# First norm by channels: x turned as it arrives, the roots spread by a matmul, and the mixer's residual read back from a stored copy

## Chip, cores, metric

The kernel runs on one core of a Trainium2 chip. The time is device microseconds of one execution; three runs of the kernel before are at hand. Beside them stands one profiled execution with its trace. The engines are PE (TensorE, matrix products), DVE (VectorE), ACT (ScalarE), POOL (GpSimd) and SP, whose queue issues most of the DMAs.

## What is computed

A stack of two residual layers over a stream of 1024 positions with 1024 channels, each layer followed by a gated feed-forward block, and a last norm. Only the beginning matters here: a norm, the input projection of the first mixer, and its output projection with the residual.

```python
def rmsnorm(x, g):
    y = x * lax.rsqrt(jnp.mean(x * x, axis=-1, keepdims=True) + EPS)
    return y * g

def even_mixer(x, w_in, ..., w_out):
    p = x @ w_in
    xa, ga, c_pre, b_post, vb = jnp.split(p, ...)        # 512 channels each
    xa = causal_depthwise_conv(xa, lru_conv_w, lru_conv_b)
    ya = rg_lru(xa, ...) * jax.nn.gelu(ga)
    yb = b_post * causal_depthwise_conv(c_pre * vb, sconv_w, sconv_b)
    return jnp.concatenate([ya, yb], axis=-1) @ w_out

h = x
h = h + even_mixer(rmsnorm(h, mix0_norm), ...)
h = h + conv_glu_ffn(rmsnorm(h, ffn_norm[0]), ...)
h = h + odd_mixer(rmsnorm(h, mix1_norm), ...)
h = h + conv_glu_ffn(rmsnorm(h, ffn_norm[1]), ...)
out = rmsnorm(h, final_norm)
```

## The kernel before, in words

**Operands.** All products take activations with channels on the 128 partitions and positions along the row: `AH` and `AL` hold, for each of eight chunks of 128 channels, the rounded high part and the rest of 1024 positions. Weights come as blocks of 1024 rows by 128 columns (512 KB) and are split in the same way into `wh` (a cast on ACT) and `wl` (a subtraction on DVE, both in L129). A block of the result is the sum of AH·wh, AL·wh and AH·wl over eight chunks: 24 products for a half of 512 positions (`proj_half`, products in L376). Weight blocks are loaded by the class `Weights` in a fixed plan (0xa0, 0ga0, 0cp0, 0vb0, 0bp0, 0xa1, ...; output blocks 0o00 to 0o07 and again 0o10 to 0o17); two raw blocks and three split pairs are held at a time, so the cast of a block waits for the last product with the block three before.

**The first norm** (class `Start`) works on x with positions on the partitions: eight tiles of 128 positions by 1024 channels. For each tile ACT squares and sums a row (`squares`, L433), DVE and ACT form the root (`root`, L438 to L442), DVE multiplies by root and gain in one pass over 1024 columns (`scale`, L446; the gain is one row broadcast to all partitions, a DMA of 512 KB, `g0`), PE turns the product in eight 128x128 transposes into two PSUM banks (`high`, L455), ACT casts the banks into AH (L459), and DVE subtracts for AL (`low`, L464). The order for the first four tiles is the string `START`; `warm` (L470) puts plain products of the identity into PE's queue. Positions 0 to 511 of the blocks xa and ga are computed in two quarters of 256 as the tiles come, then the other four tiles are worked on beside the first half of block 0cp0 (`second`, `beside`), then come the second halves of xa, ga and 0cp0.

**Behind it.** xa goes through a convolution of four taps (ACT L402, DVE L405) and is split into xh and xl (L369, L370); the gates ra and ix are products with the small gate weights gwa and gwx (L1345), which POOL clears (L1326), loads (L1330) and ACT and DVE split. 0vb and 0bp follow. Blocks of 1024 positions have two PSUM buffers (`big`), halves have four (`sml`). SBUF tiles of 128x1024 (`t4`) and 128x512 (`t2`) have four buffers each; the parameter rows, gwa and gwx, and the rows of the next stage's convolution weights are t2 tiles.

**The residual.** `out_proj0` computes the eight output blocks for positions 0 to 511, then for the rest. `residual(oc)` loads 128 channels of x (512 KB in rows of 512 bytes, L546), PE turns them in eight transposes (L550) and ACT copies the two banks into `hT` (L551), the stream with channels on the partitions. `evict` adds a block's result (L557), stores it to `hdr` in DRAM (L558) for a later stage, and squares it for the next norm.

**Order.** A planner traces the whole program and gives each engine its queue, by the order of the program among what is ready in its own model of time. An instruction inside `tc.issue_after(i)` stands behind i on the engine that the two share; it doesn't wait for i to end.

Of the kernel before, what the change touches and what calls it, by code (L numbers as in the profile page):

```python
# [16 lines left out]
P = 128  # L17
T = 1024
H = 512
# [35 lines left out]

START = "q0 r0 s0 q1 r1 s1 h0 q2 l0 r2 s2 h1 l1 w1 q3 r3 s3 h2 l2 w2 h3 l3".split()

WARM = {"h0": 3, "h1": 3}
# [25 lines left out]
class Weights:  # L84
# [12 lines left out]
    def _dma(self, n=None):  # L97
        n = n or NWST + (self.more is not None)
        while self.n_dma < min(self.n_conv + n, len(self.plan) if self.limit is None else self.limit):
# [6 lines left out]
            self.nc.sync.dma_start(w[:, :k, :m], ap)  # L106
# [13 lines left out]
    def ahead(self, depth=3):  # L120
# [14 lines left out]
        return did  # L135

# [20 lines left out]
def trunk(ctx: ExitStack, tc: tile.TileContext, x, mix0_norm, mix0_w_in, lru_conv_w, lru_conv_b,  # L157
# [258 lines left out]
    g0 = spl.tile([P, D], F32, name="g0")  # L416
    xs_, last = [], {}

    class Start:


        def __init__(self):
            self.ss = spl.tile([P, DC, 4], F32, name="sss")
            self.ys, self.ps = {}, {}

        def load(self, tt):
            xt = spl.tile([P, D], F32, tag="x", bufs=5, name=f"x{tt}")
            nc.sync.dma_start(xt, x[tt * P:(tt + 1) * P, :])
            xs_.append(xt)

        def squares(self, tt):
            y = self.ys[tt] = t4(f"xn{tt}")
            return act.activation(y, xs_[tt], AF.Square, accum_out=self.ss[:, tt, 0:1]), None  # L433

        def root(self, tt):
            sm = self.ss[:, tt]
            v, r, q = sm[:, 1:2], sm[:, 2:3], sm[:, 3:4]
            dve.tensor_scalar(v, sm[:, 0:1], 1.0 / D, EPS, op0=ALU.mult, op1=ALU.add)  # L438
            a = act.activation(r, v, AF.Abs_reciprocal_sqrt)
            dve.tensor_tensor(q, v, r, op=ALU.mult)  # L440
            dve.scalar_tensor_tensor(q, q, -0.5, r, op0=ALU.mult, op1=ALU.mult)
            return a, dve.scalar_tensor_tensor(r, q, 1.5, r, op0=ALU.add, op1=ALU.mult)  # L442

        def scale(self, tt):
            y = self.ys[tt]
            return None, dve.scalar_tensor_tensor(y, xs_[tt], self.ss[:, tt, 2:3], g0,  # L446
                                                  op0=ALU.mult, op1=ALU.mult)

        def high(self, tt):
            y, self.ps[tt] = self.ys.pop(tt), []  # L450
            for q_ in range(2):
                ps = psml(f"xp{tt}{q_}")
                for i in range(4):
                    c = 4 * q_ + i
                    pe.transpose(ps[:, i * P:(i + 1) * P], y[:, c * P:(c + 1) * P], ident)  # L455
# [11 lines left out]
        def warm(self, n):  # L467
            ps = psml("warm")
            for _ in range(n):
                pe.matmul(ps[:, :P], ident, ident, start=True, stop=True)  # L470
# [1417 lines left out]
```

## Time and profile before

| | |
|---|---|
| runs | 2139.49, 2139.52, 2137.47 us; median 2139.49 |
| profiled execution | 2138.28 us, its span 2136.6 us |
| granted PE clock, mean | 0.997 |
| PE busy | 2097.7 us (98%), 9673 products |
| DVE, ACT, POOL busy | 1599.6, 1068.9, 74.7 us |
| from HBM, to HBM | 181.93 MB, 64.26 MB |
| first product of the start (0xa) | 16.94 us |
| last product of the start (0cp0b) begins | 59.21 us |
| output projection, first product | 258.42 us |

Times in rows of the trace are us from the start of the span. A row of the timeline has start, duration, engine (PEld loads PE's stationary operand, SPq is SP's queue of DMAs), line of the kernel, operation, result<-operands, and, in brackets, how long the engine stood idle before it and what ended that. Products are pipelined: one is shown with some 0.39 us, and the next starts 0.23 us after it. A row by groups has the line, the names and shapes, count, busy time in us and mean ns. A row by stretches has the stretch, its length, busy time and instructions of PE, PEld, DVE, ACT and POOL, the granted PE clock, the DMA engines' share, and GB/s. A row of waits has who waited for whom, us in total, how often, and the longest.

### The profile page before, as it was taken

To read this page: it belongs to the slowest core of one execution; us is meant where nothing else is said; L and a number is where in the kernel's file an instruction comes from. 1 tells how busy PE (TensorE), PEld (TensorE's weight loads), DVE (VectorE), ACT (ScalarE), POOL (GpSimd) and SP (SyncE) were. 2 spreads that over 40 slices of the span, in tenths; PEclk is the share of its full clock that TensorE was granted. 3 is DMA by queue.
4 is the path that set the end of the run, shared out by engine and by line. 5 is a ranking of instruction groups with operands and counts; after the bars stand their busy time and mean duration, and the time that the engine had idled before them with its cause. 6 is when DMAs were issued, how large, how long until landed. Compare 5 with 4: busy or idle time off the path is not lost. (4 is left out here: it accounts for less than half of the span.)

```text
span 2136.6 us, 25861 instructions
## 1 busy us (share of the span) xinstructions
PE 2097.7 (98%) x9673; PEld 1721.0 (81%) x9673; DVE 1599.6 (75%) x2290; ACT 1068.9 (50%) x1493; POOL 74.7 (3%) x121
## 2 busy tenths in 40 slices
PE   8999999999999999999999999999999999999998
PEld 7888888788888878888778888788788888878887
DVE  6655647998888777876566666868998888777864
ACT  5333534654555555333556575744655545555323
POOL 0000001000000000000111111100000000000000
PEclk9999999999999999999999999999999999999999
DMA  4111342333333267751221211542233332267732
GB/s 149 57 50 43 109 150 94 101 107 109 103 108 94 79 223 248 238 168 69 75 67 46 82 48 58 165 151 89 94 116 106 104 109 95 85 234 244 232 101 79
DMA packets 269318, 249.98 MB, mean 117 GB/s; under 512 B 10224, under 2 KB 222000, under 8 KB 269192
## 3 DMA queue, kind: packets, MB, share of 16 engines
q1 hardware_dynamic: 268856, 247.83, 36.4%
q8 instruction: 76, 1.25, 0.2%
q0 software_dynamic: 192, 0.30, 0.1%
q14 instruction: 50, 0.41, 0.1%
q10 hardware_dynamic: 144, 0.20, 0.0%
HBM read 181.93 MB, written 64.26 MB: 115 GB/s over the span
## 5 line engine op out<-in xcount | busy, mean ns | idle before, releaser
L129 ACT CAST wh<-wst 128x1024 fp32r<-128x1024 f32 (+1 forms) x87 | 86.3, 992 | 222.6 <-PE op L376 45.0
L129 DVE TENSOR_TENSOR wl<-wst,wh 128x1024 fp32r<-128x1024 f32 (+1 forms) x87 | 99.9, 1148 | 96.2 <-ACT wh L129 96.0
L676 PE MATMUL X<-TH,wh 128*128 128x512 f32 x384 | 150.1, 391 | 1.8 <-ACT u L1033 1.4
L676 PE MATMUL X<-TH,wl 128*128 128x512 f32 x384 | 149.7, 390 | 0.7 <-DVE wl L370 0.7
L676 PE MATMUL X<-TL,wh 128*128 128x512 f32 x384 | 149.5, 389 | 0.0
L369 ACT CAST wh<-wst 128x1024 fp32r<-128x1024 f32 x96 | 100.3, 1051 | 75.7 <-PE YZ L676 49.5
L370 DVE TENSOR_TENSOR wl<-wst,wh 128x1024 fp32r<-128x1024 f32 x96 | 116.5, 1218 | 11.9 <-ACT wh L369 11.9
L698 DVE SCALAR_TENSOR_TENSOR cg<-g,par_c,cg 128x1023 f32<-128x1023 f32 x88 | 112.7, 1281 | 7.1 <-ACT cg L692 6.0
L698 DVE SCALAR_TENSOR_TENSOR cv<-v,par_c,cv 128x1023 f32<-128x1023 f32 (+1 forms) x88 | 112.3, 1276 | 0.1
L676 PE MATMUL YZ<-AH,wh 128*128 128x512 f32 x240 | 93.5, 389 | 0.0
L676 PE MATMUL YZ<-AL,wh 128*128 128x512 f32 x240 | 93.4, 389 | 0.0
L676 PE MATMUL YZ<-AH,wl 128*128 128x512 f32 x240 | 93.4, 389 | 0.0
L1033 ACT COPY u<-X 128x512 f32<-128x512 f32 x40 | 23.6, 589 | 136.3 <-PE X L676 136.3
L676 PEld LDWEIGHTS X<-TH,wh 128*128 128x128 f32 x384 | 72.1, 188 | 18.9 <-ACT u L1033 2.6
L676 PEld LDWEIGHTS X<-TH,wl 128*128 128x128 f32 x384 | 72.1, 188 | 16.5 <-DVE wl L370 1.6
L676 PEld LDWEIGHTS X<-TL,wh 128*128 128x128 f32 x384 | 72.1, 188 | 14.8
L376 PE MATMUL op<-AH,wh 128*128 128x512 f32 x192 | 76.3, 397 | 0.6 <-ACT hT_o L551 0.6
L376 PE MATMUL op<-AH,wl 128*128 128x512 f32 x192 | 74.8, 390 | 0.0
L376 PE MATMUL op<-AL,wh 128*128 128x512 f32 x192 | 74.8, 390 | 0.0
L692 ACT ACTIVATE cg<-g,par_c 128x1024 f32<-128x1024 f32 x44 | 54.8, 1246 | 30.0 <-DVE g L1057 25.6
L1055 DVE TENSOR_TENSOR v<-p,u 128x512 f32<-128x512 f32 x40 | 27.6, 690 | 53.9 <-ACT u L1048 53.9
L1598 ACT ACTIVATE P<-P,sm 128x128 f32<-128x128 f32 (+3 forms) x64 | 49.7, 777 | 30.0 <-DVE sm L1595 29.7
(779 smaller groups left out, 6309.3 us busy)
## 6 DMA issues: line engine op xcount, KB each, us to landing
wst<-in_ffn_up_dram SPq DMA_DIRECT2D x88, 512.0 KB
br<-hids SPq DMA_DIRECT2D x56, 512.0 KB
wst<-in_mix_w_in_dram SPq DMA_DIRECT2D x40, 512.0 KB
wst<-in_mix_w_out_dram SPq DMA_DIRECT2D x32, 512.0 KB
hids<-cv SPq DMA_DIRECT2D x32, 512.0 KB
hdr<-hT_o SPq DMA_DIRECT2D x32, 256.0 KB
hids<-t SPq DMA_DIRECT2D x32, 256.0 KB
hd<-hdr SPq DMA_DIRECT2D x16, 512.0 KB
```

What stands on the lines that cost most here:

```text
L129: did = self.nc.scalar.copy(wh[:, :k, :m], w[:, :k, :m]), self.eng.tensor_tensor(wl[:, :k, :m], w[:, :k, :m], wh[:, :k, :m].bitcast(F32), ...
L369: return (act.copy(h, src), (eng or dve).tensor_tensor(l, src, h.bitcast(F32), op=ALU.subtract))
L370: (eng or dve).tensor_tensor(l, src, h.bitcast(F32), op=ALU.subtract))
L376: last_mm = pe.matmul(ps, a[:, k], b[:, k, s], start=(k == 0 and i == 0), stop=(k == DC - 1 and i == 2))
L676: last = pe.matmul(ps, a[:, k0 + k], b[:, k], start=(first and k == 0 and i == 0), stop=(k == 3 and i == 2), skip_group_check=True)
L692: act.activation(self.cg, self.g, AF.Identity, scale=taps[2](f), bias=bias(f))
L698: dve.scalar_tensor_tensor(dst[:, dl:], src[:, :T - dl], taps[j](c), dst[:, dl:], op0=ALU.mult, op1=ALU.add)
L1033: u2_ = act.copy(u2, X)
L1055: dve.tensor_tensor(v[:, HALF[1]], p5, u3, op=ALU.add)
L1598: act.activation(Pt[:, :n], Pt[:, :n], AF.Exp, bias=low, scale=-1.0, accum_out=sm[:, 6:7])
```

## The change

x is no longer multiplied before it is turned. Each tile is turned as it lands, into `xT`, positions along the row; for the first four tiles DVE copies the banks, for the other four ACT. The squares are taken of the untouched tile as before. The roots of four tiles are formed at once (128x4); DVE lays them out as four diagonals of 128x128, and one product of a matrix of ones with them gives every partition the 512 roots (`spread`). Then, channel by channel, DVE multiplies xT by the gain (a column now, from a 4 KB load and a transpose) and the roots, ACT casts, DVE subtracts. The first halves of xa and ga are computed by channel, the AH·wl products behind the others by the table `LATE`; the turns of tiles 4 to 7 stand between them. All of this has one written order on PE, ACT and DVE (`do`). `Weights.parts` gives a block's cast and subtraction separately. xT is stored to `hdr` by halves (2 MB each), and `Out(0)` loads its residual from there in sixteen DMAs of 256 KB, as `Out(1)` did before, behind the last weight load then traced. On SP, x0 to x3 now stand ahead of the first two weight blocks, and x4 to x7 ahead of the parameter rows.

```diff
+LATE = {4: (0, 1), 5: (2, 3), 6: (4, 5), 7: (6, 7)}
...
+    def parts(self, key):
...
+        high = self.nc.scalar.copy(wh[:, :k, :m], w[:, :k, :m])
...
+        def low():
+            did = self.nc.vector.tensor_tensor(wl[:, :k, :m], w[:, :k, :m],
+                                               wh[:, :k, :m].bitcast(F32), op=ALU.subtract)
+            self._dma()
...
     class Start:
         def __init__(self):
+            self.xT = [spl.tile([P, DC, H], F32, name=f"xT{h}") for h in range(2)]
...
+        def load_g(self):
+            self.raw = t2("raw_g")[:DC, :P]
+            nc.sync.dma_start(self.raw, r1(mix0_norm))
+        def store(self, h):
+            nc.sync.dma_start(hdr[:, :, HALF[h]], self.xT[h])
...
+        def turn(self, tt, on_act):
             for q_ in range(2):
                 ps = psml(f"xp{tt}{q_}")
                 for i in range(4):
                     c = 4 * q_ + i
-                    pe.transpose(ps[:, i * P:(i + 1) * P], y[:, c * P:(c + 1) * P], ident)
+                    self.do("pe", lambda: pe.transpose(ps[:, i * P:(i + 1) * P],
+                                                       self.x[tt][:, c * P:(c + 1) * P], ident))
...
+                if on_act:
+                    self.do("act", lambda: act.copy(to, src))
+                else:
+                    self.do("dve", lambda: dve.tensor_copy(to, src))
...
+        def root(self, h):
...
+            d = self.diag = t2(f"diag{h}")
+            self.tt_(d.rearrange("p (n t) -> p n t", n=4),
+                     ident.unsqueeze(1).broadcast_to([P, 4, P]),
+                     r.unsqueeze(2).broadcast_to([P, 4, P]), op=ALU.mult)
+        def spread(self, h):
+            self.r = psml(f"rb{h}")
+            self.mm_(self.r, self.one, self.diag, start=True, stop=True)
+        def scaled(self, h, c):
+            y = self.y[c] = t2(f"y0{h}{c}")
+            self.stt_(y, self.xT[h][:, c], self.g[:, c:c + 1], self.r, op1=ALU.mult)
+            self.do("act", lambda: act.copy(AH[:, c, HALF[h]], y))
+        def low(self, h, c):
+            self.tt_(AL[:, c, HALF[h]], self.y.pop(c), AH[:, c, HALF[h]].bitcast(F32),
+                     op=ALU.subtract)
...
+        def run(self, pxa, pga, pcp):
+            lows = []
             self.warm(14)
+            for tt in range(4):
+                self.squares(tt)
+                self.turn(tt, False)
+                if tt == 0:
+                    self.gain()
+                self.warm(2)
+            self.root(0)
+            ws = []
+            for key in ("0xa0", "0ga0"):
+                with tc.issue_after(last["act"].ins):
+                    w, last["act"], low = W.parts(key)
+                ws.append(w)
+                lows.append(low)
+            self.warm(10)
+            self.spread(0)
+            self.warm(10)
+            self.scaled(0, 0)
+            self.scaled(0, 1)
+            both = list(zip((pxa, pga), ws))
+            for c in range(DC):
+                self.low(0, c)
+                if c + 2 < DC:
+                    self.scaled(0, c + 2)
+                if c in (1, 3):
+                    self.do("dve", lows.pop(0))
+                for p_, w in both:
+                    self.products(p_[:, HALF[0]], w, 0, (c,), (0, 1))
+                if c in LATE:
+                    for p_, w in both:
+                        self.products(p_[:, HALF[0]], w, 0, LATE[c], (2,))
+                if c % 2:
+                    self.turn(4 + c // 2, True)
+                if c in (2, 4, 6, 7):
+                    self.squares({2: 4, 4: 5, 6: 6, 7: 7}[c])
+            with tc.issue_after(last["act"].ins):
+                wc, last["act"], low = W.parts("0cp0")
+            self.do("dve", low)
+            self.store(0)
+            self.root(1)
+            self.products(pcp, wc, 0, range(5), (0, 1, 2))
+            self.spread(1)
+            self.products(pcp, wc, 0, range(5, DC), (0, 1, 2))
+            self.scaled(1, 0)
+            self.scaled(1, 1)
+            for c in range(DC):
+                self.low(1, c)
+                if c + 2 < DC:
+                    self.scaled(1, c + 2)
+                for p_, w in both:
+                    self.products(p_[:, HALF[1]], w, 1, (c,), (0, 1, 2))
+            self.store(1)
             turn_rows(*par_rows)
...
     class Out:
         def __init__(self, ly):
-            if ly:
+            with tc.issue_after(W.last.ins):
                 for s in HALF:
                     for c in range(DC):
                         nc.sync.dma_start(self.hT[:, c, s], hdr[:, c, s])
-        def residual(self, oc):
...
     def out_proj0(y_rest):
-        o_.residual(0)
         for oc in range(DC):
             w = W.get(f"0o0{oc}")
-            if oc < DC - 1:
-                o_.residual(oc + 1)
```

156 lines of the change are left out of this document (67 added, 89 removed).

## Prediction

> **What bounds the kernel now.** I read the page's busy shares first, then the busy time by stretches of the span, then the waits of the matrix engine in the first 64 us and around the output projection, and only then the order of instructions in these two places.
>
> ```profile
> PE 2097.7 (98%) x9673; PEld 1721.0 (81%) x9673; DVE 1599.6 (75%) x2290; ACT 1068.9 (50%) x1493; POOL 74.7 (3%) x121
> 0.00:16.90 16.90, 11.19 (x64) 10.55 (x65) 8.55 (x21) 10.27 (x22) 4.46 (x13) 0.89 0.79 234
> 16.90:42.70 25.80, 23.61 (x163) 21.79 (x161) 17.41 (x38) 13.16 (x28) 0.00 (x0) 0.94 0.46 146
> 42.70:237.00 194.30, 194.30 (x854) 159.98 (x854) 106.57 (x109) 71.83 (x77) 0.00 (x0) 1.00 0.17 50
> 255.00:300.00 45.00, 44.26 (x228) 36.80 (x228) 27.79 (x40) 21.55 (x35) 0.00 (x0) 1.00 0.59 177
> ```
>
> PE is busy in 98% of the span and without a gap from 42.7 to 237 us. So the change is worth what it takes off PE's own queue, plus the time by which it moves the end of PE's first products. Both are read from two stages: the start up to the end of the block 0cp0b, and the eight output blocks from 255 to 300 us.
>
> ```profile
> 16.94 0.56 PE L376 MATMUL 0xa<-AH,wh 128*128 128x256 f32 x1
> 54.23 0.39 PE L376 MATMUL 0cp0b<-AL,wh 128*128 128x512 f32 x1
> 59.21 0.40 PE L376 MATMUL 0cp0b<-AH,wl 128*128 128x512 f32 x1
> PE 0cp0a L376 <- DVE AL L464: 2.0, 1, 2.0
> ```
>
> The first product starts at 16.94. The last of the start stage starts at 59.21, the 23rd from the one at 54.23, so one 512-wide product takes (59.21-54.23)/22 = 0.226 us of PE and the stage ends at 59.44. It holds 144 such products, 32.6 us. The rest is the wait for data, transposes and one 2.0 us stall.
>
> **The change, the start.** Every engine's start work now stands in one written order, so I follow it by durations.
>
> ```profile
> 1.53 5.63 PE L470 MATMUL warm<-ident 128*128 128x128 f32 x28 [1.53 <-POOL ident masks.py:199]
> 8.95 0.83 PE L470 MATMUL warm<-ident 128*128 128x128 f32 x6
> 40.43 1.91 PE L455 MATMUL xp<-ident,xn 128*128 128x128 f32 x16
> 313.60 1.02 PE L344 MATMUL ms_no<-ss_no,ones 128*128 128x512 f32 x2
> 6.68 1.28 DVE L446 SCALAR_TENSOR_TENSOR xn<-x,sss,g 128x1024 f32<-128x1024 f32 x1 [0.26 <-DMA g<-in_mix_norm_dram]
> 11.63 1.06 ACT L433 ACTIVATE xn<-x 128x1024 f32<-128x1024 f32 x1 [0.70 <-DMA x<-in_x_dram]
> 17.52 0.14 DVE L438 TENSOR_SCALAR sss<-sss 128x1 f32<-128x1 f32 x1
> 18.32 0.16 DVE L442 SCALAR_TENSOR_TENSOR sss<-sss 128x1 f32<-128x1 f32 x1
> L464 DVE TENSOR_TENSOR AL<-xp,AH 128x512 fp32r<-128x512 f32 x16 | 10.1, 682 | 5.2 <-ACT AH L459 5.2
> 318.87 1.42 DVE L355 SCALAR_TENSOR_TENSOR hT_o<-hT_o,par_a,r_no 128x512 f32<-128x512 f32 x2
> L129 DVE TENSOR_TENSOR wl<-wst,wh 128x1024 fp32r<-128x1024 f32 x5 | 6.1, 1219 | 0.1
> L459 ACT CAST AH<-xp 128x512 fp32r<-128x512 f32 x16 | 8.4, 593 | 3.2 <-PE xp L455 3.2
> L433 ACT ACTIVATE xn<-x 128x1024 f32<-128x1024 f32 x8 | 8.5, 1062 | 5.3 <-DMA x<-in_x_dram 5.2
> L129 ACT CAST wh<-wst 128x1024 fp32r<-128x1024 f32 x6 | 6.3, 1054 | 7.4 <-PE 0ga L376 3.1 <-PE 0xa L376 2.8 <-PE 0cp0b L376 0.9
> ```
>
> Arrival: the 512 KB broadcast of the gain leaves the SP queue (a 4 KB load takes its place) and the weight block 0xa0 moves behind x3. So x1 takes the place of the gain (used at 6.68) and x3 that of x2 (used at 11.63). x4 to x7 go ahead of the eleven small loads of parameter rows, which nothing needs before the convolution. PE can't use them sooner: the 14 warm matmuls hold it to 7.16, then come four turns of eight transposes (0.96 each, half of 1.91), each with two warm matmuls (four instructions, 0.5), the gain's transpose (0.2) and ten warm ones (2.3): 15.5. DVE's last copy out of PSUM is done near 13.9 (0.68 each by the AL row, the nearest with 512 columns read from PSUM; not below the 0.16 of the smallest operation, and what it gave PE's queue would hide), the root takes 1.0 (17.52 to 18.48), and the diagonal, between the same bounds and taken at 0.68, is done at 15.6. The spreading matmul is like the one at 313.60, 1.02: 16.7. Then one chunk of DVE (0.70), its cast on ACT (0.59) and its low part on DVE (0.68): PE starts at 18.1, 1.1 us later than now, and the low operand follows at 18.8.
>
> First half: xa and ga are 96 products there (48 in each half), and the first half's 48 are 10.9 us with four turns of 0.97: 14.8. DVE has to deliver eight channels, each 0.66 for the product (half of 1.42, less what overlaps) and 0.60 for the low part, and two weight lows of 1.2. It sets the pace of the first four channels: low parts at 18.8, 20.0, 22.4 and 23.7 against 0.9 of PE work each. Waits there and at channel 4 come to 2.4. PE ends turn 7 at 35.2.
>
> The gap that is new: behind turn 7 the queue of ACT holds two copies (0.59), the square of x7 (1.06 with 0.19 for its sum) and the cast of the third weight block (1.05). The cast is done at 38.0, its low part on DVE (1.22) at 39.3. PE idles 2.8, does two products, idles 0.8. Root 1 waits behind that low part on DVE and is covered by the 13 products left of 15. The second spread ends at 43.3, nine products cover the first channel's chain, then come 48 products (0.28 more per channel than DVE needs) to 56.3 and 24 for 0cp0b to 61.75. Against 59.44 that is **+2.3**. The terms: 1.1 later at the first product, turns and spread 4.9, waits 6.1, products the same; what goes are the transposes, the stall of 2.0 and the slow clock of the old start.
>
> **After the start.** Now xa ends 5.2 us before ga, and its convolution runs under ga and 0cp0b; after the change both end together.
>
> ```profile
> 48.99 1.05 ACT L129 CAST wh<-wst 128x1024 fp32r<-128x1024 f32 x1 [2.85 <-PE 0xa L376]
> 54.21 1.28 DVE L405 SCALAR_TENSOR_TENSOR xc<-0xa,par_a,xc 128x1021 f32<-128x1021 f32 x1
> 58.57 1.22 DVE L370 TENSOR_TENSOR xl<-xc,xh 128x1024 fp32r<-128x1024 f32 x1 [0.99 <-ACT xh L369]
> ```
>
> From the end of xa (the cast at 48.99 waited for it) to the last tap (55.49) are 6.5 us, so the bank of xa is free at 62.8 with 0cp0b done at 61.75; ga's bank may be free a little sooner. A stall of 0 to 1.0 if 0vb stands ahead of the gates in PE's queue. If the gates stand first it is 3.3 to 5.4: they need xl, which comes a cast (1.0) and 1.2 after the taps, 65.0, or as now 10.8 us after xa (59.79-48.99), 67.1. I take **+0.6**, since their order is made by a planner that fills PE with what is ready.
>
> **The residual.** 64 transposes and 16 evictions leave the output stage.
>
> ```profile
> 255.95 1.91 PE L550 MATMUL xr<-ident,xc 128*128 128x128 f32 x16
> 258.42 0.50 PE L376 MATMUL op<-AH,wh 128*128 128x512 f32 x1 [0.55 <-ACT hT_o L551]
> 261.61 1.22 DVE L129 TENSOR_TENSOR wl<-wst,wh 128x1024 fp32r<-128x1024 f32 x1
> 262.74 5.50 DVE L370 TENSOR_TENSOR AL<-Y,AH 128x512 fp32r<-128x512 f32 x9
> 264.05 1.04 PE L550 MATMUL xr<-ident,xc 128*128 128x128 f32 x8
> 264.84 0.48 PE L376 MATMUL op<-AH,wh 128*128 128x512 f32 x1
> ```
>
> A later group of eight takes 0.79 of PE's queue (264.05 to 264.84): six groups, 4.75. The first sixteen and a wait, 2.47 (255.95 to 258.42), cover something: the last low operand of block 0 is the first of the nine at 262.74, done at 263.4, and the block ends at 264.05. Without the transposes PE arrives earlier and waits for DVE, so I count 0.15 there. That cover would be worth up to 2.47 if DVE's order moves the operand forward. **-4.9**, between -4.75 and -7.2. The new cost is two stores of 2 MB in the start and sixteen loads of 256 KB that stand on SP behind the fourth output weight load. At the stage's 177 GB/s they would be 24 us; now 4.2 MB of x, half in the same stage, come by the same queue. The first is needed by the first eviction at 264 and the next every 5.4 us, so I cost them at nothing; if they come only when the first mixer's buffers are free (256), a first load that took 8 us would begin to cost. ACT's 16 copies were not on the path.
>
> Sum: 2.3 + 0.6 - 4.9 = **-2.0**. The profiled execution took 2138.28 us, so 2136.3 for it; it lies 1.2 below the median of the runs. Taken from the median, 2139.49, the forecast is **2137.5**. From here to the end PE's chain only shifts.
>
> **The clock, and the rivals.**
>
> ```profile
> 9.69:13.10 3.41, 1.17 (x11) 1.11 (x11) 3.04 (x8) 2.31 (x5) 0.00 (x0) 1.00 1.12 297
> 13.00:14.00 1.00, 1.00 (x7) 0.94 (x6) 0.63 (x6) 0.83 (x3) 0.00 (x0) 0.55 1.09 334
> 19.00:20.00 1.00, 1.00 (x7) 1.00 (x7) 1.00 (x2) 0.80 (x1) 0.00 (x0) 0.54 0.74 250
> 33.57:36.98 3.41, 2.14 (x9) 1.80 (x10) 3.01 (x5) 0.00 (x0) 0.00 (x0) 1.00 0.19 56
> ```
>
> *The clock falls in the new gap.* After a stretch with PE busy 1.17 of 3.41 us the granted clock fell to 0.50 at 13.1 and stayed there to 19.9 (0.55 and 0.54 are the means of the microseconds in which it changed); after one with 2.14 busy of 3.41 it did not. The new stretch from 35.2 to 39.3 has 0.45 busy in 4.1, so a 3.41 us stretch around it holds 0.5 to 1.6: mostly below the row that fell, or near it. The price is half the work of some 4.4 us, 2.2 us: -2.0 + 2.2 = +0.2, 2139.7. Chance 0.22, no change to be measured either way. The Trainium skill (TensorE: Matmul & The Clock Gate, "Part 1: The HAM clock gate") has the clock return to half only after an idle window of about 3.4 us; by that rule neither gap (2.8 and 0.8 us) drops it and the sum stays -2.0. This trace speaks against so strict a rule: the drop at 13.1 followed a stretch in which PE was busy a third of the time.
>
> *The start costs nothing.* If the written order runs as tightly as PE's queue allows, 0cp0b ends by 59.4, and the whole of the residual's PE time counts: -4.9 to -7.2, 2132.3 to 2134.6; I name 2134.2. For it: x arrives earlier without the broadcast, and after turn 3 only small operations are left. Against it: DVE's pace in the first channels and ACT's queue behind turn 7. Chance 0.26. It decides if PE's gap behind turn 7 is below 1 us.
>
> *The gate weights come late.* This is the one that ends slower.
>
> ```profile
> 1.43 0.53 POOL L1326 MEMSET gwa<- 128x512 f32 x1
> gwa<-in_lru_wa_dram POOLq DMA_DIRECT2D x2, 64.0 KB, 7.1
> gwx<-in_lru_wx_dram POOLq DMA_DIRECT2D x2, 64.0 KB, 7.3
> SPq L275 <- PE pt L283: 11.1, 1, 11.1
> ```
>
> They use the ring of four half-size buffers (t2). SP waited 11.1 us with a later user of that ring until the parameter rows, an earlier one, had been transposed: places are handed on in the order of the work. The change puts 19 new tiles into that ring ahead of the gate weights (the gain's rows, two diagonals, sixteen products), so their memset moves from 1.43 to about the low part of channel 4 or 5 of the second half (45.4 and 1.3 for each channel): 50.6 and 51.9. With POOL's issues and 7.3 us to land, gwx is there near 61.5. If their casts stand in ACT's queue ahead of xa's convolution, that starts at 62.2 behind two casts, not at 57.3: +4.9, both banks are late, PE idles 5 us, and the clock falls (2.2). -2.0 + 5 - 0.6 + 2.2 = +4.6, 2144.1. It decides if the landing takes over 4 us; at 7.3 the start-up's full queues were beside it, and at 50 us they are not, so I hold a landing of 3 to 4 us for likelier. Chance 0.13.
>
> **How the numbers follow.** Forecast 0.39 (its own range 2135.5 to 2139.5), clock 0.22, start for free 0.26, gate weights 0.13. A difference of 0.2% (4.3 us) is about what a measurement of this kernel can tell from none: forecast and clock lie within it, so faster 0.26, same 0.61, slower 0.13. The range takes in the free start and stops short of the worst of the gates: 2133.0 to 2143.0.
>
> **What would show it.** PE's first product at 18.1; low parts of the first four channels at 18.8 to 23.7; an idle PE for 2.8 us before 0cp0a, with ACT's cast of the third block as its releaser; the last product of 0cp0b near 61.5; the granted clock there 1.00 or 0.50; no xr rows, and output blocks 5.44 us apart from block 1 on; block 0 still waiting for its last low operand. The prediction is wrong if PE stands idle for over 3 us between 0cp0b and 0vb, if an eviction waits for a load of hdr, or if the start ends before 59.4.

## The result, and the profile after

| kernel | runs, us | median |
|---|---|---|
| before | 2137.47, 2137.48, 2139.49, 2139.52 | 2138.48 |
| after | 2161.80, 2165.32, 2165.38, 2166.36 | 2165.35 |

The change makes the kernel 1.2% slower: ratio 1.0122, 95% interval 1.0110 to 1.0134, some 27 us. The forecast was 2137.5 with a range up to 2143.0, and none of its rivals comes near.

The page of the changed kernel has the loss in its first line. PE makes 63 products fewer than before and is busy 32 us longer (2097.7 before), at a granted clock that is no lower. The second fence has the stretches of the start and of the output blocks, as in the prediction's fence for before.

```profile
PE 2130.1 (98%) x9610; PEld 1713.0 (79%) x9610; DVE 1609.5 (74%) x2285; ACT 1064.3 (49%) x1479; POOL 75.7 (3%) x122
```

```profile
0.00:18.00 18.00, 16.40 (x120) 15.57 (x120) 8.49 (x18) 10.15 (x19) 1.00 (x8) 1.00 0.87 294
18.00:37.50 19.50, 16.00 (x83) 12.18 (x82) 10.74 (x17) 12.90 (x24) 0.00 (x0) 1.00 0.59 179
37.50:61.80 24.30, 23.77 (x99) 18.16 (x99) 18.07 (x33) 12.09 (x19) 3.80 (x6) 1.00 0.42 132
61.80:237.00 175.20, 174.36 (x747) 139.78 (x747) 98.68 (x96) 59.12 (x60) 0.00 (x0) 1.00 0.17 48
255.00:300.00 45.00, 44.81 (x194) 35.66 (x193) 34.14 (x45) 20.25 (x29) 0.00 (x0) 1.00 0.64 205
```

The start looks as forecast: first product at 18.0, a gap behind 37.5 at a clock of 1.00, no transposes xr. The fourth row is the odd one. PE is as full as before, but 747 products took 174.36 us; before, 854 took 194.30 in a longer stretch, 0.2275 us for each against 0.2334. The groups of the feed-forward block, where the change touches nothing, say the same (before, then after: line, operation, count, then shortest/median/longest in ns):

```profile
L676 PE MATMUL YZ<-AH,wh x240: 389/389/436, 392.1 to 1894.4; 128*128 128x512 f32 x120
L676 PE MATMUL YZ<-AL,wh x240: 388/389/397, 392.3 to 1894.6; 128*128 128x512 f32 x120
```

```profile
L759 PE MATMUL YZ<-AH,wh x240: 393/396/408, 395.8 to 1918.8; 128*128 128x512 f32 x120
L759 PE MATMUL YZ<-AL,wh x240: 392/394/397, 396.0 to 1919.0; 128*128 128x512 f32 x120
```

Not the mean moved but all of them: the shortest product after is longer than the median before. Read by stages (starts of the named products in the trace, us; in the last two columns kernels that are explained below) the loss is everywhere and grows with the number of products. 0g is the first block of the first feed-forward block (FFN), X and YZ are products of an FFN's body, dq and dp those of its down projection, 1q is the first block of the second mixer. TH and TL, below, are a split operand of the FFN like AH and AL, dh and dl split weights of it.

| stage | before | after | before_short | after_pad_b |
|---|---|---|---|---|
| span's start to the last 0bp | 255.7 | 264.4 | 260.7 | 258.7 |
| last 0bp to the first 0g (output blocks) | 96.9 | 91.3 | 98.7 | 89.4 |
| first X to first dq (first FFN's body) | 404.3 | 412.0 | 411.9 | 407.7 |
| first dq to first 1q | 223.0 | 225.2 | 227.1 | 224.0 |
| first 1q to last op (second mixer) | 466.1 | 470.5 | 469.3 | 466.3 |
| last op to the second FFN's first dq | 428.7 | 435.5 | 435.5 | 430.5 |
| from there to the last dp | 179.1 | 180.8 | 181.1 | 183.0 |

### The profile page after: what moved, and what is told of

Same layout as the page of the kernel before. It is cut to its first block, busy times and chain, and to the rows that moved or that the text cites. A ratio compares the mean times of both kernels' runs of the same rounds, so it can differ in the third digit from the quotient of the medians.

```text
span 2163.6 us, 25732 instructions
## 1 busy us (share of the span) xinstructions
PE 2130.1 (98%) x9610; PEld 1713.0 (79%) x9610; DVE 1609.5 (74%) x2285; ACT 1064.3 (49%) x1479; POOL 75.7 (3%) x122
## 3 DMA queue, kind: packets, MB, share of 16 engines
q1 hardware_dynamic: 264776, 251.50, 36.3%
q8 instruction: 75, 1.23, 0.2%
## 5 line engine op out<-in xcount | busy, mean ns | idle before, releaser
L759 PEld LDWEIGHTS X<-TL,wh 128*128 128x128 f32 x384 | 72.2, 188 | 16.3
L759 PE MATMUL YZ<-AH,dh 128*128 128x512 f32 x160 | 63.4, 396 | 0.0
```

Of the source, the lines that this page charges most:

```text
L759: last = pe.matmul(ps, a[:, k0 + k], b[:, k], start=(first and k == 0 and i == 0), stop=(k == 3 and i == 2), skip_group_check=True)
```

## Experiments: where the tiles lie

The built program shows one thing that the diff does not. The change takes the eight rows of the first gain out of `par_a`, a small tile of parameters, which falls from 96 to 88 columns, and each tile placed behind it in SBUF moves down by 32 bytes: wh and wl, TH and TL, dh and dl among them. AH and AL stand ahead of it and stay. In the kernel before, all of these start at the same place within 256 bytes (192); after, the weights start at 160 and AH and AL still at 192. The theory: a product is slower when its moving and its stationary tile lie apart in this way. The first rival: something in the change's schedule or traffic does it. Two kernels tell them apart, the change with the tiles put back, and the kernel before with the tiles moved and nothing of the change.

**after_pad**

```diff
         t = cp.tile([P, n], F32, name=f"par_{name}")
+        if name == "a":
+            cp.tile([P, 8], F32, name="pad")
```

> The changed kernel with an unused pad of 8 columns behind par_a, so that par_a and the pad take the 384 bytes that par_a took before, and every tile placed behind it in SBUF starts where it starts in the kernel before. Nothing else differs from the changed kernel. Theory (address): the loss of 26.9 us comes from the 32 bytes by which the weight tiles wh and wl and all tiles behind them moved when the eight norm rows left par_a; a product takes 234 ns from start to start in place of 227 when its moving and its stationary tile no longer start at the same place within 64 bytes. It expects 2136 to 2140 us, the change's own worth, and 227 ns. Rival (schedule): the loss comes from what the change does (the store of xT, the loads of hdr, the new order of the start), which the pad leaves alone. It expects 2162 to 2167 us and 234 ns.

**before_short**

```diff
-        (r1(mix0_norm), 8), (lru_conv_w[0].rearrange("k (c p) -> (k c) p", p=P), 16),
+        (lru_conv_w[0].rearrange("k (c p) -> (k c) p", p=P), 16),
...
```

> The kernel before without the eight rows of mix0_norm in par_a, which nothing there reads: par_a falls from 96 to 88 columns, one small load of rows goes, and all tiles behind par_a move down by 32 bytes. Nothing of the change is in it. Theory (address): 2162 to 2169 us, as much as the changed kernel lost, with products of AH and AL at 234 ns. Rival (schedule): 2136 to 2141 us and 227 ns.

Measured: after_pad 1.0009 of the kernel before (0.9997 to 1.0021), before_short 1.0127 (1.0111 to 1.0144). One edit of 32 bytes takes the loss away, the same 32 bytes bring it into a kernel without the change. The group of products, for after_pad and then before_short:

```profile
L761 PE MATMUL YZ<-AH,wh x240: 389/389/436, 389.6 to 1898.8; 128*128 128x512 f32 x120
```

```profile
L676 PE MATMUL YZ<-AH,wh x240: 392/396/412, 399.4 to 1923.0; 128*128 128x512 f32 x120
```

Is it the start of a tile, or the distance of the two? Two more kernels move AH and AL by 32 bytes, once with all other tiles and once alone.

**before_all32** and **before_ah32** (the second has the edit of before_short as well, so that only AH and AL move)

```diff
+    cp.tile([P, 8], F32, name="pad")
     AH = cp.tile([P, DC, T], F32R, name="AH")
```

> The kernel before with a pad of 32 bytes ahead of AH: AH, AL, the weight tiles, TH, TL and all behind them start at 32 bytes past a multiple of 64, all together. Theory A (only the distance of the two operands counts): moving and stationary tile still start at the same place within 64 bytes, so 2136 to 2145 us (up to 5 us for what X's products lost at 32 and 32 in the changed kernel) and 227 ns for products of AH. Theory B (a tile that starts off a multiple of 64 costs by itself): 2165 us or more, 234 ns for nearly all products.

> The kernel before with a pad of 32 bytes ahead of AH and with par_a at 88 columns, so that AH and AL alone move up by 32 bytes and the weight tiles and all tiles behind stay where they are in the kernel before. Theory A (the distance of the two operands counts): every product of AH or AL with a weight tile is slow, some 5,600 of them by 6.6 ns, so 2162 to 2175 us, 234 ns. Theory C (the start of the stationary tile alone counts): 2136 to 2141 us, 227 ns. Theory B (any tile off a multiple of 64) expects the same as A here, and is told from A by the kernel in which all tiles move.

Measured: before_all32 1.0015 (1.0005 to 1.0024), before_ah32 1.0129 (1.0112 to 1.0146). The same AH at the same place is fast in one and slow in the other; so it is the distance, and a tile off a multiple of 64 costs nothing by itself. That settles theory A against B and C. The group of products, for before_all32 and then before_ah32:

```profile
L677 PE MATMUL YZ<-AH,wh x240: 389/389/435, 393.7 to 1900.9; 128*128 128x512 f32 x120
```

```profile
L677 PE MATMUL YZ<-AH,wh x240: 393/396/412, 399.5 to 1923.1; 128*128 128x512 f32 x120
```

Two kernels for the period of the distance went less cleanly.

**before_wl32** (a pad between the wh and the wl tiles, and one behind them)

```diff
+        if n == 0:
+            wh = self.pool.tile([P, DC, P], F32R, tag="wh", bufs=3, name="wh0")
+            self.pool.tile([P, 8], F32, name="pad")
+            return [wh, self.pool.tile([P, DC, P], F32R, tag="wl", bufs=3, name="wl0")]
...
+    tmp.tile([P, 8], F32, name="pad2")
```

> The kernel before with a pad of 32 bytes between the three wh tiles and the three wl tiles of the weight pool and another behind them: the low parts wl alone start 32 bytes past a multiple of 64 there; AH, AL, TH, TL and wh stay at multiples of 64 (the pair wh2x, wl2x that the down projection's pool lends stays whole). A group of products goes (wh,AH), (wh,AL), (wl,AH). Theory N (a product is slow when the stationary tile that is loaded for the next one lies 32 bytes off the moving tile that is streaming): the step from (wh,AL) to (wl,AH) takes 234 ns, the other two 227. Theory O (when the product's own two tiles lie 32 bytes apart): the step from (wl,AH) to the next takes 234 ns, the other two 227. Both expect 8 to 13 us above the kernel before, a third of what moving all weights cost.

**before_ah16**

```diff
-    AH = cp.tile([P, DC, T], F32R, name="AH")
-    AL = cp.tile([P, DC, T], F32R, name="AL")
+    AH, AL = (cp.tile([P, DC * T + 8], F32R, name=n)[:, 4:4 + DC * T]
+              .rearrange("p (c t) -> p c t", c=DC) for n in ("AH", "AL"))
```

> The kernel before with AH read and written from 16 bytes and AL from 48 bytes past a multiple of 64, all weight tiles and TH, TL at multiples of 64. Theory 64 (any distance within 64 bytes costs alike): AH's and AL's products take 234 ns, 2162 to 2175 us. Theory 32 (only the half of 64 bytes in which the two start counts): AH's products stay at 227, AL's take 234, 8 to 13 us. Theory linear (the loss grows with the distance): AH's products 230, AL's 237 or 230.

Measured: 1.0137 (1.0122 to 1.0152) and 1.0181 (1.0164 to 1.0198). Both expectations failed. In before_wl32 the step from AL·wh to AH·wl is the slowest as theory N has it (YZ: 237.7 ns from start to start), but the step from AH·wh, between tiles that didn't move, takes 232.1, and only the third is near 227 (229.0): one odd load of three costs as much as three. So neither theory says which of the tiles in flight must agree, and that stays open. And my pads came to 64 bytes, so TH and dh lay 64 from AH, and AH with dh was slow too (233.1 ns): a distance of 64 is not free, the period is longer than I had written. In before_ah16 the two wider tiles moved the weights by 64 bytes as well, so its distances within 256 are 48 and 16 and it tests none of its three theories; it shows that these distances cost too.

**before_wp128** (the pad of after_pad, 32 columns wide, in the kernel before)

> The kernel before with 32 unused columns behind par_a: the weight tiles, TH, TL and all tiles behind par_a move up by 128 bytes, AH and AL stay. The kernel with the low parts 32 bytes off showed products of AH and dh, which lay 64 bytes apart within 128, at 233 ns, so 64 is too short a period. Theory 128 (products are fast when both tiles start at the same place within 128 bytes): 227 ns, 2138 to 2144 us. Theory 256: AH's and AL's products at 233 ns or more, 2162 to 2180 us.

Measured: 1.0108 (1.0093 to 1.0123), theory 256. In the table are the mean spacings from one 512-wide product to the next (starts in the trace, those of 200 to 260 ns) for products with wh, wl, dh or dl, by the distance of moving and stationary tile within 256 bytes:

| kernel | AH, AL: distance, ns | TH, TL: distance, ns | ratio to before |
|---|---|---|---|
| before | 0, 227.5 | 0, 226.9 | |
| after | 32, 233.3 | 0, 228.9 | 1.0122 |
| after_pad | 0, 227.5 | 0, 226.9 | 1.0009 |
| before_short | 32, 233.3 | 0, 228.9 | 1.0127 |
| before_all32 | 0, 227.5 | 0, 226.9 | 1.0015 |
| before_ah32 | 32, 233.3 | 0, 228.9 | 1.0129 |
| before_wp128 | 128, 232.6 | 0, 227.7 | 1.0108 |

In the kernel before AH (byte 17,600) and the first wh (93,120) lie an odd multiple of 256 apart, 295 of them, so 256 is a whole period. The 5,400 products of AH and AL at 5.8 ns and 2,100 of TH and TL at 2.0 are 35 us; the ratio has 27. Some of the rest is waiting that slower products hide. PE's gaps of over 0.26 us in the two FFNs' bodies come to 9.0 us more than the usual spacing before and to 5.8 after, and DVE's waits for weight loads in the first FFN fall from 12.6 to 4.0 us.

```profile
DVE s L648 <- DMA wst<-in_ffn_up_dram: 12.6, 13, 2.2
```

```profile
DVE s L731 <- DMA wst<-in_ffn_up_dram: 4.0, 6, 2.0
```

(The waits of DVE between X's first product and the first dq, before and after: us in total, times, longest.) Why products with TH, at distance 0, take 228.9 beside slow ones isn't settled: those of X, which alternate with products of AH, take 229.7; those of dqB, which stand among themselves, 226.9 as before.

## Experiments: what the change is worth without that

**after_pad_b** (after_pad once more)

> The changed kernel with the pad of 8 columns once more, in five rounds, as the base of the two kernels beside it. The prediction's sum (start +2.3, residual -4.9, after the start +0.6) expects 2.0 us under the kernel before, a ratio of 0.9991; the rival that the clock falls to 0.50 in the gap behind turn 7, as the first run of this kernel showed at 38.1 us, expects +0.2 us, 1.0001.

**after_oldres** (the padded kernel, with `residual` as it was)

```diff
-            self.store(0)
...
-            self.store(1)
...
-            with tc.issue_after(W.last.ins):
+            if ly:
                 for s in HALF:
...
+        o_.residual(0)
         for oc in range(DC):
             w = W.get(f"0o0{oc}")
+            if oc < DC - 1:
+                o_.residual(oc + 1)
```

> The padded changed kernel with the residual part undone: mixer 0's output block loads x by column and turns it on PE again (64 transposes xr, copied by ACT), and the stores of xT to hdr and the loads from it are gone; the start stays changed. Theory (the residual is worth what the prediction says): 4.9 us above the padded changed kernel, a ratio of 0.0023 more to the kernel before, and the whole residual gain shows between op's first product and the first 0g. Rival (the transposes were hidden, or hdr's traffic costs as much as they): within 1 us of the padded changed kernel.

**after_early**

```diff
+                if c == DC - 1:
+                    with tc.issue_after(last["act"].ins):
+                        wc, last["act"], low = W.parts("0cp0")
+                    self.do("dve", low)
                 if c % 2:
                     self.turn(4 + c // 2, True)
...
-            with tc.issue_after(last["act"].ins):
-                wc, last["act"], low = W.parts("0cp0")
-            self.do("dve", low)
```

> The padded changed kernel with the cast of 0cp0's weights (ACT's wh, DVE's wl) issued ahead of turn 7 in place of behind the squares of tile 7, so that the first products of 0cp0a find them ready. Theory (the gap behind turn 7 is waited for on the path): the wait of 2.7 us for wh and that of 0.5 us for wl go, and the time falls by 2.7 to 3.2 us against the padded changed kernel, 5 us where the clock no longer falls there. Rival: the wait only moves to AL or to the second spread, and the time falls by less than 1 us.

Measured: after_pad_b 1.0008 (0.9999 to 1.0017), after_oldres 1.0008 (0.9999 to 1.0016), after_early 0.9989 (0.9980 to 0.9997) and, once more on another chip (after_early_b), 0.9998 (0.9989 to 1.0007).

> The padded changed kernel with the early cast of 0cp0's weights, once more, as the base of the kernel beside it: 0.998 to 0.9997 of the kernel before, the first FFN at 407 us from X's first product to the first dq.

after_early does what was expected: the waits for wh and wl behind turn 7 are gone, its first product of 0cp0a starts at 34.45 in place of 37.12, the last 0bp 3.1 us earlier, and on the same chip it is 4 us under after_pad_b. after_oldres is a puzzle. Its output blocks take 96.8 us against 89.4, so the new residual is worth 7.4 there, more than forecast; and still its time is that of after_pad_b. In its profile the clock fell for 6.8 us in the start. But it also does better behind the start: its first FFN takes 405.2 us, after_pad_b's 407.7, with the same instructions in the same order on ACT, DVE and PE. One more run of the kernel before gave a profile to set beside these:

> The kernel before itself, for a profile from this chip, to set the stages of the kernels beside it against: X's first product at 375.7 us and 227 ns from product to product, as in the profile shown.

Its first FFN takes 405.5 us, and X starts at 375.2. DVE's waits for weights in that stage are 16.3 us there, 14.6 in after_oldres, 18.6 in after_pad_b. They differ at a few loads, and there the trace has something else on the DMA rings. The DMA queues of after_pad_b from 598 to 603 us (packets, MB, share of 16 engines), and the wait of DVE that ends there:

```profile
q1 hardware_dynamic: 1228, 0.88, 60.0%
q8 instruction: 1, 0.02, 1.5%
```

```profile
L733 DVE TENSOR_TENSOR s<-wst x1: 693/693/693, 603.2 to 603.2; 128x512 f32<-128x512 f32 x1
...
  DMA wst<-in_ffn_up_dram: 2.7, 1
```

The same load in before_look, from 601.5 to 606.2 us, and the wait that ends there:

```profile
q1 hardware_dynamic: 1320, 1.05, 72.3%
```

```profile
L648 DVE TENSOR_TENSOR s<-wst x1: 692/692/692, 606.2 to 606.2; 128x512 f32<-128x512 f32 x1
...
  DMA wst<-in_ffn_up_dram: 1.5, 1
```

A packet of an instruction queue, 16 KB and 0.9 to 1.9 us long in that stage, stands among the 512-byte packets of the load; in before_look the stretch has none and the wait is 1.2 us shorter. These packets come every 26 to 33 us. The page of after has 75 of them with 1.23 MB, and PE has 9610 products and as many weight loads: 64 bytes each, if they are PE's instructions, 256 in a packet. The 64 transposes xr were 128 instructions, half a packet, and indeed the packets of after_pad_b come half a period off: 20.9, 52.4, 78.7, 110.0 us behind X's first product against 3.2, 34.8, 67.6, 95.6 in before_look and 2.6, 34.6, 67.2, 92.8 in after_oldres. Theory (fetch): these packets hold up weight loads, and the change moved them to where a load is being waited for. It can be tested by giving PE 128 instructions more, in the changed kernel and in the kernel before.

**pad_fill** (behind turn 7)

```diff
+        def fill(self, n, ps):
+            for _ in range(n):
+                self.do("pe", lambda: pe.transpose(ps[:, :DC], ident[:DC, :], ident[:DC, :DC]))
...
+            self.fill(64, psml("fill"))
             self.products(pcp, wc, 0, range(5), (0, 1, 2))
```

> The padded changed kernel with 64 transposes of 8 columns of ident, whose result nothing reads, in the gap on PE behind turn 7. They put back the number of instructions that the 64 transposes xr took from PE's stream (a transpose is a weight load and a product). In the padded kernel's profiles 16 KB packets of an instruction queue, of about 1 us each, run at 110, 228, 286 and 345 us after the first FFN's first product, and DVE's next wait for a weight load is 0.8 to 1.8 us longer than in the kernels whose packets run half a period earlier (96, 123, 153 ...). Theory (fetch): the 64 transposes move the packets back by half a period, the first FFN takes 405 us in place of 408 from X's first product to the first dq, and the whole time falls by 3 to 7 us against the padded changed kernel, to 0.998 of the kernel before or less. Rival (the loss comes from hdr's transfers or from chance): the first FFN still takes 407.5 to 408.5 us and the time stays within 1.5 us of the padded changed kernel.

**before_fill** (in `warm` of the kernel before, called with 14, 3 and 3)

```diff
                 pe.matmul(ps[:, :P], ident, ident, start=True, stop=True)
+            for _ in range({14: 16}.get(n, 24)):
+                pe.transpose(ps[:, :DC], ident[:DC, :], ident[:DC, :DC])
```

> The kernel before with 64 transposes of 8 columns of ident, whose result nothing reads, behind the warm-up products of the start, where PE waits for x. Theory (fetch): the instruction packets move by half a period onto the weight loads, the first FFN takes 407 to 408.5 us, and the whole time grows by 2 to 6 us, a ratio of 1.001 to 1.003. Rival: within 1 us of the kernel before, the first FFN at 404 to 405.5 us.

**early_fill** (after_early, with the `fill` of pad_fill)

```diff
-            self.warm(14)
+            self.warm(6)
+            self.fill(80, psml("fill"))
```

> The padded changed kernel with the early cast of 0cp0's weights, and with eight of the first 14 warm-up products replaced by 80 transposes of 8 columns, which makes 128 instructions more on PE (a warm-up product is two weight loads and two products). Theory (fetch): the packets move by half a period, the first FFN takes 405 us, and the time is 3 to 7 us under that kernel without them (0.9989 of before), 0.9955 to 0.9975 of the kernel before. Rival: 0.998 to 0.9995.

**early_short** (after_early; the second number of `warm` counts products over 64 columns)

```diff
-            self.warm(14)
+            self.warm(10, 8)
...
-                self.warm(2)
+                self.warm(0, 4)
...
-            self.warm(10)
+            self.warm(0, 20)
             self.spread(0)
-            self.warm(10)
+            self.warm(0, 20)
```

> The same with 32 of its 42 warm-up products (128 columns, two weight loads and two products each) replaced by twice as many of 64 columns, 128 instructions more on PE and as many columns streamed. Theory (fetch): the instruction packets move by half a period, the first FFN takes 405 us, the start stays within 1 us, and the time is 2 to 6 us under the kernel beside it, 0.996 to 0.9985 of the kernel before. Rival: the time is within 1 us of the kernel beside it, or the start loses what the first FFN gains.

**early_gap** (after_early)

```diff
-                    self.products(p_[:, HALF[0]], w, 0, (c,), (0, 1))
+                    self.products(p_[:, HALF[0]], w, 0, (c,), (0,))
+                    if c in (1, 3) and p_ is pxa:
+                        self.do("pe", lambda: fill(pcp, 12))
+                    self.products(p_[:, HALF[0]], w, 0, (c,), (1,))
...
+                if ly == 0 and f in (2, 3):
+                    fill(X, 20)
                 prod(X, w["a"], 0, "11")
```

> The padded changed kernel with the early cast of 0cp0's weights and 64 transposes of 8 columns in waits that PE has: twelve each behind the products of channels 1 and 3 of the first half (where PE waits for the low part) and twenty each ahead of the first products of two blocks of the first FFN. Theory (fetch): the instruction packets fall half a period earlier, the first FFN and the second take 5 us less together than without the transposes (405 and 428.5 us), the start loses at most 1 us, and the time is 0.9965 to 0.9985 of the kernel before. Rival: 0.999 to 1.0005.

| kernel | ratio to before | first packets behind X, us | first FFN | second FFN |
|---|---|---|---|---|
| before_look | (one run) | 3.2, 34.8, 67.6, 95.6 | 405.5 | 428.9 |
| before_fill | 1.0025 (1.0015 to 1.0035) | 20.9, 52.4, 81.0, 110.2 | 408.1 | 431.5 |
| after_pad_b | 1.0008 (0.9999 to 1.0017) | 20.9, 52.4, 78.7, 110.0 | 407.7 | 430.5 |
| pad_fill | 0.9993 (0.9983 to 1.0004) | 3.5, 35.4, 67.6, 96.7 | 406.2 | 428.4 |
| after_early_b | 0.9998 (0.9989 to 1.0007) | 20.9, 52.5, 78.8, 110.2 | 408.5 | 432.0 |
| early_fill | 0.9999 (0.9991 to 1.0008) | 2.9, 34.6, 67.1, 93.0 | 404.6 | 428.0 |
| early_short | 0.9989 (0.9980 to 0.9998) | 2.9, 35.2, 67.7, 96.2 | 405.5 | 428.2 |
| early_gap | 0.9974 (0.9960 to 0.9989) | 14.1, 36.3, 69.7, 98.4 | 408.0 | 427.6 |

The mechanism holds in both directions and in each of the five: where the packets come at 110 us, the two FFNs take 838.2 to 840.5 us together, where they come at 93 to 98, 832.6 to 835.6. (early_gap's first FFN contains 40 of the small transposes.) In before_fill the same place as above shows the packet and the wait of after_pad_b:

```profile
q8 instruction: 1, 0.02, 1.4%
```

```profile
L650 DVE TENSOR_TENSOR s<-wst x1: 691/691/691, 606.6 to 606.6; 128x512 f32<-128x512 f32 x1
...
  DMA wst<-in_ffn_up_dram: 2.5, 1
```

In time, before_fill and early_gap came out in the ranges that were expected; pad_fill, early_fill and early_short missed theirs, because they lost in the start. In pad_fill the 64 transposes outlast the gap (0cp0a begins at 40.24 in place of 37.12) and the last 0bp is 4.7 us later than in after_pad_b. In early_fill the 80 transposes took 8.7 us, 0.109 each, far more than the eight warm-up products whose place they took. In early_short the start is 6.5 us longer than in after_early_b: its products over 64 columns follow one another after 0.110 us, those over 128 columns there after 0.112. early_gap puts the transposes where PE waits, and there the sum comes out: it is the version that beats both kernels, 0.26% under the one before.

This answers part of the puzzle of after_oldres. Its profiled execution (2147.8 us, the slowest of its runs) is 3.7 us behind that of after_pad_b. It loses the 7.4 us of the residual and 2.8 in the start, where its clock fell, but gains 2.5 and 2.1 in the two FFNs' bodies, where its packets come half a period earlier, and 4.1 in the last down projection, on which more below. So most of what the new residual gains in its own stage is lost again behind it.

## Why the prediction was wrong, step by step

**The step that failed** is its last sentence on the sum, "From here to the end PE's chain only shifts". It took 0.226 us for a product from the trace of before and held it for a property of the engine; it is one of a program whose tiles lie at equal places within 256 bytes. A change that removed eight columns of one small tile broke that. The runs show 0.233 us in its place, and some 27 us with it. No view of the profile of before shows it, and the diff shows it only to someone who asks what lies behind par_a. None of the prediction's three signs of being wrong came either: in the changed kernel PE waits 0.6 us between 0cp0b and 0vb, no eviction waits for hdr, and the start ends later than 59.4.

With the tiles put back the forecast's own terms can be checked. One profile stands for each kernel; the two of the kernel before (before and before_look) differ by up to 1.9 us in a stage. The views are those of after_pad_b, whose clock was 1.00 in this stretch; waits first, then the timeline.

```profile
PE 0cp0a L481 <- ACT wh L140: 2.7, 1, 2.7
PE 0vb L393 <- ACT gg L1438: 0.7, 1, 0.7
PE 0xa L481 <- DVE AL L475: 0.7, 2, 0.3
PE 0cp0a L481 <- DVE wl L145: 0.5, 1, 0.5
PE ra L1416 <- ACT xh L386: 0.3, 1, 0.3
```

```profile
17.27 0.69 DVE L475 TENSOR_TENSOR AL<-y,AH 128x512 fp32r<-128x512 f32 x1
18.53 0.69 DVE L475 TENSOR_TENSOR AL<-y,AH 128x512 fp32r<-128x512 f32 x1
20.93 0.69 DVE L475 TENSOR_TENSOR AL<-y,AH 128x512 fp32r<-128x512 f32 x1
22.19 0.69 DVE L475 TENSOR_TENSOR AL<-y,AH 128x512 fp32r<-128x512 f32 x1
...
33.82 0.60 PE L498 MATMUL xp<-ident,x 128*128 128x128 f32 x4
37.12 0.50 PE L481 MATMUL 0cp0a<-AH,wh 128*128 128x512 f32 x1 [2.71 <-ACT wh L140]
41.48 1.02 PE L481 MATMUL rb<-diag,one 128*128 128x512 f32 x2
...
60.89 0.39 PE L393 MATMUL 0cp0b<-AH,wl 128*128 128x512 f32 x1
62.02 0.50 PE L393 MATMUL 0vb<-AH,wh 128*128 128x512 f32 x1 [0.74 <-ACT gg L1438]
...
258.74 0.39 PE L393 MATMUL 0bp<-AH,wl 128*128 128x512 f32 x1
258.96 0.39 PE L393 MATMUL op<-AH,wh 128*128 128x512 f32 x1
259.95 0.50 PE L393 MATMUL op<-AL,wh 128*128 128x512 f32 x1 [0.60 <-DVE AL L387]
```

- *The start, +2.3.* Low parts end at 18.0, 19.2, 21.6 and 22.9, in the forecast spacing and 0.8 earlier. PE is shown idle for only 0.7 us before them, but a product is shown with 0.39 us where the next can start 0.23 behind it; from start to start the products around them lose 2.2, against 2.4. Turn 7 ends at 34.4 (35.2), the gap is 2.7 and 0.5 (2.8 and 0.8) with the releasers named, the second spread ends at 42.5 (43.3), and the last product of the start begins at 60.89, 1.7 later than the 59.21 of before and 2.2 later than the 58.74 of before_look. Right, up to 0.6 too dear.
- *After the start, +0.6.* The last 0bp begins at 258.74 against 255.7: +3.0 in all, so +1.3 here, a wait of 0.74 for gg among it. Start and rest together, forecast +2.9, measured +3.0 (+3.5 against before_look).
- *The residual, -4.9.* The stage took 89.4 in place of 96.9, -7.5, outside the bounds that I gave. Block 0 does wait for its last low part, but 0.6 us, where I had nearly the whole 2.47 covered: 1.9 are gained. The six later groups are worth the other 5.6, 0.93 each and not the 0.79 read from one of them. No eviction waits for hdr.
- *The sum.* At the first 0g after_pad_b stands at 348.1, the kernel before at 352.6 (before_look 352.1): -4.5, where -2.0 was forecast. That is near the rival in which the start costs nothing, for another reason than it gave. The rest of the way gives it back: by the stages of the first table +3.4 and +1.8 in the two FFNs' bodies and +3.9 in the last down projection. So even with the tiles put back the forecast gain isn't there: the two sets of runs are at 1.0009 and 1.0008 of the kernel before, where 0.9991 was forecast. The first two losses are the packets. The third stage takes 178.6 to 184.9 us in the kernels whose operands are not apart, 181.6 in before_all32. Of its 3.9, 2.0 stand in one place: before its block dq114A PE waits 3.4 us for DVE in place of 1.4, and DVE had waited 4.3 us for the load of x12110B in place of 2.3. before_all32 has the long waits too (3.2 and 4.1), after_early_b, with packets as in after_pad_b, has not (1.1 and 2.0); so neither the change nor the place of the packets behind X explains them, and what delays that load stays open.
- *The clock.* It stayed at 1.00 behind turn 7 in the profiles of after and after_pad_b and fell to 0.50 in those of after_pad (at 38.1, for 3.4 us) and after_oldres, which has the same start (at 36.9, for 6.8 us). From the first product of 0cp0a to the last of 0cp0b the four take 24.2, 23.8, 24.7 and 26.0 us, so against after_pad_b the fall cost 1.0 and 2.2 us; the price was 2.2. So this rival comes in some executions. The Trainium skill's rule (TensorE: Matmul & The Clock Gate, "Part 1: The HAM clock gate"), by which the gap would be too short to drop it, holds for two of these four.
- *The gate weights* were in time: PE's only wait there is for gg.

## What to carry to other kernels

A kernel that is bound by PE can lose over 1% by where its tiles lie, so before costing a change ask which small tile it resizes and what is placed behind it, and keep the size (a pad) unless the distance of moving and stationary operands stays a multiple of 256 bytes. When every product of one shape has moved by the same few ns, in stages that the change doesn't touch, look for such a cause first, and test it by making the same move in the kernel before. A gain early in the program is only kept if the later stages have slack against their loads; the number of PE instructions removed also decides where the fetches of instructions fall.

## What the runs showed of the hardware

- Products of 512 columns: 227.5 ns from start to start where moving and stationary tile have the same place within 256 bytes, 232.6 to 233.3 where they lie 32 or 128 apart. Distances of 16, 48 and 64 were slow too. Beside products that lie apart, products at the same place are slow as well (228.9 for TH in after, 232.1 for AH·wh in before_wl32). What in the chip makes it was not looked into.
- Instruction packets of 16 KB take 0.9 to 1.9 us on the DMA rings, and the wait for a load of 512-byte packets was 2.5 and 2.7 us with one among them, 1.5 without.
- In one execution small transposes kept PE busy in the trace and not its clock. In pad_fill PE was busy in all of 34.5 to 38.0, from 35.45 on with 8-column transposes, and the granted clock fell to 0.50 at 38.4 for 6.8 us (the stretches of that kernel):

```profile
34.50:38.00 3.50, 3.50 (x50) 3.33 (x49) 0.00 (x0) 2.88 (x5) 0.00 (x0) 1.00 0.19 67
38.00:45.20 7.20, 7.20 (x38) 6.11 (x37) 2.48 (x6) 0.38 (x2) 0.00 (x0) 0.53 1.03 328
```
